# Value projections of a float32 transformer: 512 weight columns per matmul instead of 256

## The chip, the cores and the metric

The kernel runs on one core of a Trainium2 chip. The metric is device time in microseconds (us) from the start to the end of one execution. TensorE (PE) multiplies, VectorE (DVE) and ScalarE (ACT) do the elementwise work, GpSimd (POOL) some small steps, SyncE (SP) issues the loads. Matmul results land in PSUM, which has eight banks of 512 float32 columns on 128 partitions.

## The reference

One program of float32 work on x of 256 tokens by 1024 features. First a swiglu layer, token mixing and a second swiglu layer; then two blocks of attention and a squared-ReLU layer with layer norms, scaled and shifted by `c` through `ada_w`. The parts that the change touches are the projections to values:

```
# token mixing
rq, rk, rv, rg, nq, nk, nv, g_ret, g_na = split(u @ w_in, ...)   # rv 1024 wide, nv 512 wide
y    = bidirectional_retention(q, k, heads(rv, 256), ...)        # 4 heads
y_na = neighborhood_attention(nq, nk, nv, rel_bias) @ w_na_out   # 8 heads of 64
# first attention (16 heads of 64, causal; one block of 256 holds all tokens)
q, k, v = split(h @ w_in, 3)                                     # 1024 wide each
# second attention (8 heads, two maps of 64 each)
q, k, v = split(h @ w_in, 3)
w = softmax(q1 k1^T) - lam * softmax(q2 k2^T)
o = rms_norm(w @ v, subln_g) * (1 - lambda_init)                 # per head, 128 wide
out = o @ w_out
```

## The kernel before

Activations lie with features on the partitions, as X[128, 8, 256]: eight chunks of 128 features by 256 tokens. Every float32 operand is split into two float32r parts (H and L, or wh and wl), and one product becomes three: wh·XH, wh·XL, wl·XH (`mmA`, `mmB`).

Weights stream from DRAM in slots of 1 MB, each [128, 2048] in the buffer `raw`, four buffers deep, loaded by SP in one fixed order (the list `ws`). ScalarE copies half a slot to wh (L109), VectorE subtracts it for wl (L90); the halves lie in a ring of seven. The `tick()` after each half's products moves this stream on by a half and lets each waiting generator (`bg`) issue its next step: the heads of an attention are generators (`pair`), begun a number of ticks after their projection (`WAITS`, `NA_WAITS`, `RET_WAITS`). So the order on every engine is the order in which the program issues, and ticks are its clock.

Most projections (`proj`) hold weights still and move 256 tokens: the result has features on the partitions. Values are wanted with tokens on the partitions, so `projA` (L461) holds 128 tokens of X still and moves 256 weight columns. A slot has all 1024 rows of 256 columns; each half (512 rows) takes 24 products, for two token blocks, into the two halves of one bank. There are 14 such slots: four rv and two nv in mixing, four in each attention. ScalarE then copies the bank's two halves to SBUF (L1621 in the attentions), and `vdone` (`nvdone`) tells the heads that their values are there.

PSUM has two pools of four banks, `gu` and `acc`. Attention's pairs of heads take scores (as), transposed probabilities (at) in `acc`; the product with the values (ao) goes to a `gu` bank, or, once `tail` is set, to an `acc` bank, since the four banks of the output projection (oacc) take `gu` then. `QKV` sets the order of an attention's projections: (1, i) is queries and keys of two pairs of heads, (0, i) a slot of values. In the second attention a pair ends with Squares of ao on ScalarE (L1575), a sum s on VectorE (L545), a power r on POOL (L540), a product r and the scaled o on VectorE (L1579, L1581), two transposes of o on PE (L1585), and YH on ScalarE (L1591), YL on VectorE (L1592), the moving input's counterpart for the output projection (`down`, `down_tail`).

```
461  def projA(bank, XH, XL):
463      for h, (wh, wl) in enumerate(st.use(n, 256)):
466              for k in range(4):
467                  mmA(two(bank)[:, t], wh[:, k], wl[:, k], XH[:, 4 * h + k, ts], ...)
470          tick()
```

Of the kernel before, what the change touches and what calls it, by code (L numbers as in the profile page):

```python
# [16 lines left out]
D = 1024  # L17
# [16 lines left out]
# the order of the parts of an attention (1 for queries and keys, 0 for values; of which heads), after how  # L34
# many steps of the stream a pair of heads starts, and from which pair on two of its steps are one
QKV = (((1, 0), (0, 0), (0, 1), (1, 1), (1, 2), (1, 3), (0, 2), (0, 3)),
       ((1, 0), (0, 0), (1, 1), (1, 2), (0, 1), (1, 3), (0, 2), (0, 3)))
# [5 lines left out]
# the sums whose last products wait for the gap between two parts  # L43
# [6 lines left out]
class Stream:  # L50
    """Weights in the order of their use: loaded ahead, split into two float32r parts ahead."""
# [70 lines left out]
    def quarter(self, n, q):  # L122
        """A quarter of slot n, the first of which come before any others."""
        h, c = q // 2, slice(q % 2 * 512, q % 2 * 512 + 512)
        if q % 2 == 0:
            self.parts[n, h] = tuple(self.pool.tile([128, 1024], F32R, name=i, bufs=RING) for i in ("wh", "wl"))
        wh, wl = self.parts[n, h]
        raw = self.raw[n][:, q * 512:(q + 1) * 512]
        self.nc.scalar.activation(wh[:, c], raw, AF.Copy)  # L129
        return lambda: self.nc.vector.tensor_tensor(wl[:, c], raw, wh[:, c].bitcast(F32), OP.subtract)  # L130
# [10 lines left out]
    def ahead(self):  # L141
        """The next half of a slot, when it is a weight's."""
        if self.si in self.wpos and 2 * self.next_pos() < self.done + RING:
            self.piece(None)

    def use(self, n, b):
        """Slot n in two halves of its rows; each as its two parts, b columns wide."""
        while self.next_pos() <= n + 0.5:
            self.piece()
        self.flush()  # L150
        return [[t.rearrange("p (k f) -> p k f", f=b) for t in self.parts[n, h]] for h in range(2)]
# [10 lines left out]
def block_kernel(ctx, tc, A, out):  # L162
# [22 lines left out]
    def rev(t):  # L185
        """[128, 2, 256] of a tile, every 64 of a row backwards."""
        v = t[:, 63:64]
        return bass.AP(tensor=v.tensor, offset=v.offset, ap=[list(v.ap[0]), [S, 2], [64, 4], [-1, 64]])
# [4 lines left out]
    # ---- small tensors  # L193
# [31 lines left out]
    # ---- the order of the weights  # L225
    def cols(w, c0, k=KB, n=256):
        return ("w", w[:, c0:c0 + n].rearrange("(k p) f -> p k f", p=128), n)

# [28 lines left out]
    for i in range(2):  # L257
        ws.append(cols(wm, 256 * i))
        ws.append(cols(wm, 512 + 256 * i))
        for j in (2 * i, 2 * i + 1):  # L260
            ws.append(cols(wm, 1024 + 256 * j))
        for j in (2 * i, 2 * i + 1):
            ws.append(cols(wm, 2048 + 256 * j))
    for i in range(2):
        for b in (3072, 3584, 4096):
            ws.append(cols(wm, b + 256 * i))
    for i in range(4):
        ws.append(cols(wm, 4608 + 256 * i))
        ws.append(cols(A["w_ret_out"], 256 * i))
# [7 lines left out]
    for l, (wi, wo) in enumerate((("moba_w_in", "moba_w_out"), ("diff_w_in", "diff_w_out"))):  # L277
        for f, i in QKV[l]:
            for b in ((0, D) if f else (2 * D,)):
                ws.append(cols(A[wi], b + 256 * i))  # L280
        for i in range(4):
            ws.append(rws(A[wo], 256 * i))
        mlp_slots(A["mlp_w_up"][l], A["mlp_w_down"][l])
# [18 lines left out]
    # ---- adaLN modulation: columns of silu(c) @ ada_w + ada_b  # L302
# [24 lines left out]
    def ada_cols(o, t):  # L327
        """The sums over the partitions, of three bfloat16 parts that hold all of a float32."""
        pool, bufs = adap[-1]
        parts = [pool.tile([128, D], BF16, name=f"ada{i}", bufs=bufs) for i in range(3)]  # L330
        SC.activation(parts[0], t, AF.Copy)  # L331
        yield 1
        GP.tensor_tensor(t, t, parts[0], OP.subtract)  # L333
        yield 2
        SC.activation(parts[1], t, AF.Copy)
        yield 1
        GP.tensor_tensor(parts[2], t, parts[1], OP.subtract)
        ada_now.clear()
        ada_out.append((o, parts))
        if o // 8 in HELD:  # L340
            return
        yield 4
        ada_mm()
        yield 1
        ada_end()
# [3 lines left out]
    @contextmanager  # L349
    def ada_pool(n):  # L350
        """Room for the parts of n sums at once."""
        with tc.tile_pool(name="ada", bufs=1) as pool:
            adap.append((pool, n))
            yield
            ada_drain()
            ada_mm()
# [5 lines left out]
    def gap(p, n):  # L362
        """In the gap between two parts: products of a sum that waited for it, or of no use."""
        if ada_out:
            ada_mm(acc, 1)
            if not ada_out:
                start(ada_later(), 1)
            n -= 12
        warm(p, n)
# [48 lines left out]
    # ---- matrix products; a product of two float32 is three of their float32r parts  # L418
# [42 lines left out]
    def projA(bank, XH, XL):  # L461
        n = nxt()
        for h, (wh, wl) in enumerate(st.use(n, 256)):
            for t in range(2):
                ts = slice(t * 128, (t + 1) * 128)
                for k in range(4):
                    mmA(two(bank)[:, t], wh[:, k], wl[:, k], XH[:, 4 * h + k, ts], XL[:, 4 * h + k, ts],
                        h == 0 and t == 0 and k == 0, h == 1 and k == 3)
            st.release(n, h)
            tick()  # L470
# [35 lines left out]
    # ---- float32 into two float32r parts  # L506
# [4 lines left out]
    # ---- statistics over the features  # L511
    def stat(p):
        """What Stat left in a bank, by token."""
        return p[:, 0:128].rearrange("p (t c) -> p t c", c=64)[:, :, 0]

    class Stat:
        """Sums over the features of eight chunks, 64 like columns for 128 tokens; six of them are added up first."""
# [30 lines left out]
    def warm(p, n):  # L548
        """Products that nobody reads, for TensorE's clock not to fall while it waits."""
# [13 lines left out]
    class PostRms:  # L563
# [36 lines left out]
        def finish(self, coef, eps=RMS_EPS):  # L600
            """X += coef * rms_norm, by two chunks, and the next input of it."""
# [40 lines left out]
    class PostLn:  # L642
# [41 lines left out]
        def stats(self, means):  # L684
            """1/deviation by token; means(mean) once the mean is there."""
# [10 lines left out]
        def finish(self):  # L696
            """The next input, by two chunks, and what the residual needs: v - mean and 1/deviation."""
# [50 lines left out]
    class Ahead(PostLn):  # L748
        """A layer norm before products that take its input as x * a: what they lack is applied to their results."""
# [35 lines left out]
        def steps(self):  # L785
            """The statistics, the mean and 1/deviation by token on all partitions, the residual."""
# [21 lines left out]
        def proj(self, alloc):  # L808
            """x * a times 256 columns: the product, and that of -a and c."""
# [18 lines left out]
        def result(self, o, t):  # L828
            """The whole product but for what is to be added by feature."""
# [7 lines left out]
    class Last(PostLn):  # L837
        """The last layer norm: turned to tokens by rows before the statistics are known."""
# [83 lines left out]
    class Input:  # L922
        """The input of a part in two parts: x * a + c, a and c by feature."""
# [41 lines left out]
    class Next(Input):  # L965
        """The input of a part that normalizes after its first product: X * gain, and its statistics."""
# [37 lines left out]
    # ---- parts  # L1004
# [128 lines left out]
    # ---- start: x, transposed  # L1133
# [9 lines left out]
    def first_pair(banks, XH, XL):  # L1143
        """The first product, in the order in which its quarters come from DRAM."""
# [58 lines left out]
    # ---- token mixing  # L1203
    def mixing(nx):
        with tc.tile_pool(name="mix", bufs=1) as mp:
# [136 lines left out]
            for i in range(2):  # L1342
# [21 lines left out]
                for j in (2 * i, 2 * i + 1):  # L1364
                    b = gu("rv")
                    projA(b, XH, XL)
                    for t in range(2):
                        SC.activation(rv[:, t, j * 256:(j + 1) * 256], two(b)[:, t], AF.Copy, scale=nx.r[:, t:t + 1])
                    vdone.add(j)
# [9 lines left out]
            for i in range(2):  # L1379
# [10 lines left out]
                b = gu("nv")  # L1390
                projA(b, XH, XL)
                for t in range(2):
                    SC.activation(nv[:, t, i * 256:(i + 1) * 256], two(b)[:, t], AF.Copy, scale=nx.r[:, t:t + 1])
                nvdone.add(i)
# [53 lines left out]
    # ---- second block  # L1448
# [31 lines left out]
    def attention(l, nx, gate, follow):  # L1480
        with tc.tile_pool(name=f"att{l}", bufs=1) as mp:
# [115 lines left out]
            def room(n):  # L1597
                """Waits until n of the banks that products of attention go through are free."""
# [18 lines left out]
            def vv(i):  # L1617
                b = gu("v")
                projA(b, XH, XL)
                for t in range(2):  # L1620
                    SC.activation(vt[:, t, i * 256:(i + 1) * 256], two(b)[:, t], AF.Copy)  # L1621
                vdone.add(i)

            for f, i in QKV[l]:
                if not f and i == 2:
# [23 lines left out]
    def after_ln(l, i):  # L1649
        """The input of the part after a layer norm, and the residual from it."""  # L1650
# [89 lines left out]
```

## Time and profile before

| | us |
|---|---|
| median of three runs | 1287.78 (1287.3 to 1287.98) |
| profiled execution | 1287.8 |
| its span | 1287.8 |
| PE busy | 1262.7 (98%) |
| PE weight loads, beside the products | 1244.6 (97%) |
| VectorE busy | 1046.8 (81%) |
| ScalarE busy | 672.0 (52%) |
| POOL busy | 280.5 (22%) |

The profiled execution is one run of the program, and its span covers all of it. Busy times of an engine add up its instructions where they do not overlap. In the rows a PE product's own duration is longer than its step to the next one, since products overlap: 96 products with durations near 282 ns can take 11.39 us.

### The profile page before, as it was taken

Reading aid. Unit: us, or ns where it says so; the run is one execution under the profiler, and the core shown is the slowest. Engines: PE = TensorE matmul, PEld = TensorE weight load, DVE = VectorE, ACT = ScalarE, POOL = GpSimd, SP = SyncE. Lnnn points to the kernel's source line nnn. Section 1 sums busy time; section 2 is a strip of 40 time slices with the busy share of each in tenths; the row PEclk is TensorE's granted clock in tenths of the full one; section 3 lists DMA queues with packets and bytes.
Section 4 is the critical chain, followed back from the end, with each engine's and each line's share of the span. In section 5 each row is a group of like instructions: output and inputs, shape, how many; then the busy total and the mean of one; then the engine's idle time right before and its main releaser. Section 6 shows DMA issues by size and latency. Waiting matters only on the chain.

```text
span 1287.8 us, 25632 instructions
## 1 busy us (share of the span) xinstructions
PE 1262.7 (98%) x10768; PEld 1244.6 (97%) x10768; DVE 1046.8 (81%) x1437; ACT 672.0 (52%) x1070; POOL 280.5 (22%) x204
## 2 busy tenths in 40 slices
PE   9999999999999999999999999979999999999998
PEld 9999999999999999999999999979999999999997
DVE  5999867887776589887588759999969987998864
ACT  5454445656544365354465546545536565565542
POOL 1011104221000130011110017423322003832311
PEclk9999999999999999999999999989999999999999
DMA  8787974874566348877535335878753543677630
GB/s 300 264 309 256 317 244 90 268 240 149 200 226 212 116 164 301 303 279 262 164 111 186 131 99 188 270 271 281 260 171 113 183 132 103 225 250 234 202 134 33
DMA packets 176659, 265.25 MB, mean 206 GB/s; under 512 B 10432, under 2 KB 145952, under 8 KB 176544
## 3 DMA queue, kind: packets, MB, share of 16 engines
q1 hardware_dynamic: 169824, 261.53, 60.1%
q10 hardware_dynamic: 6720, 2.10, 0.9%
q8 instruction: 84, 1.38, 0.4%
q14 instruction: 31, 0.25, 0.1%
HBM read 262.56 MB, written 1.05 MB: 205 GB/s over the span
## 4 chain that ended last, share of the span: by engine, by line
PE 86%; DVE 8%; POOL 2%; issue 1%; ACT 1%; DMA 0%; DVEq 0%; SPq 0%; POOLq 0%; ACTq 0%
PE acc L191 24%; PE u L191 20%; PE g L191 12%; PE v L191 3%; PE q L191 3%; PE k L191 3%; PE oacc L191 2%; DVE wl L90 2%; PE yr L191 2%; PE rg L191 2%; PE rv L191 2%; PE as L191 1%; PE ao L191 1%; PE pst L191 1%; PE nk L191 1%
## 5 line engine op out<-in xcount | busy, mean ns | idle before, releaser
L90 DVE TENSOR_TENSOR wl<-raw,wh 128x1024 fp32r<-128x1024 f32 x392 | 515.2, 1334 | 24.3 <-ACT wh L109 23.9
L109 ACT ACTIVATE wh<-raw 128x1024 fp32r<-128x1024 f32 x392 | 403.6, 1052 | 130.3 <-PE u L191 32.2
L191 PE MATMUL acc<-HL,wh 128*128 128x256 f32 x864 | 243.9, 282 | 0.0
L191 PE MATMUL acc<-HH,wl 128*128 128x256 f32 x864 | 243.7, 282 | 0.0
L191 PE MATMUL acc<-HH,wh 128*128 128x256 f32 x864 | 242.8, 281 | 0.0
L191 PE MATMUL u<-XH,wh 128*128 128x258 f32 (+1 forms) x864 | 201.6, 285 | 0.4 <-ACT wh L129 0.4
L191 PE MATMUL u<-XL,wh 128*128 128x258 f32 (+1 forms) x864 | 200.7, 284 | 0.0
L191 PE MATMUL u<-XH,wl 128*128 128x258 f32 (+1 forms) x864 | 200.2, 283 | 0.0
L191 PEld LDWEIGHTS acc<-HH,wh 128*128 128x128 f32 x864 | 163.9, 190 | 0.0
L191 PEld LDWEIGHTS acc<-HH,wl 128*128 128x128 f32 x864 | 162.4, 188 | 0.0
L191 PEld LDWEIGHTS acc<-HL,wh 128*128 128x128 f32 x864 | 161.9, 187 | 0.0
L191 PEld LDWEIGHTS u<-XH,wh 128*128 128x128 f32 x864 | 145.7, 191 | 0.7 <-ACT wh L129 0.6
L191 PEld LDWEIGHTS u<-XH,wl 128*128 128x128 f32 x864 | 146.0, 191 | 0.1
L191 PEld LDWEIGHTS u<-XL,wh 128*128 128x128 f32 x864 | 145.1, 190 | 0.0
L191 PE MATMUL g<-XH,wh 128*128 128x256 f32 x480 | 133.5, 284 | 1.6 <-ACT XH L942 1.3
L191 PE MATMUL g<-XL,wh 128*128 128x256 f32 x480 | 133.2, 283 | 1.0 <-DVE XL L618 0.9
L191 PE MATMUL g<-XH,wl 128*128 128x256 f32 x480 | 132.7, 282 | 0.0
L320 DVE SCALAR_TENSOR_TENSOR adacc<-raw,csil,adacc 128x1024 f32<-128x1024 f32 x84 | 118.2, 1408 | 1.7
L834 POOL TENSOR_TENSOR a<-a,RB 128x512 f32<-128x512 f32 x32 | 68.0, 2125 | 170.7 <-DVE a L833 169.9
L333 POOL TENSOR_TENSOR adacc<-adacc,ada 128x1024 f32<-128x1024 f32 x12 | 27.7, 2311 | 329.3 <-ACT ada L331 254.3
L191 PEld LDWEIGHTS g<-XH,wh 128*128 128x128 f32 x480 | 89.5, 189 | 2.7 <-ACT XH L942 2.0
L191 PEld LDWEIGHTS g<-XL,wh 128*128 128x128 f32 x480 | 89.5, 189 | 1.6 <-DVE XL L618 1.1
(368 smaller groups left out, 2643.0 us busy)
## 6 DMA issues: line engine op xcount, KB each, us to landing
raw<-in_ada_w_dram SPq DMA_DIRECT2D x48, 1024.0 KB, 5.7
raw<-in_ffn_w_in_dram SPq DMA_DIRECT2D x42, 1024.0 KB, 6.8
raw<-in_mlp_w_up_dram SPq DMA_DIRECT2D x32, 1024.0 KB, 5.4
raw<-in_mlp_w_down_dram SPq DMA_DIRECT2D x32, 1024.0 KB, 5.0
raw<-in_w_mix_in_dram SPq DMA_DIRECT2D x26, 1024.0 KB, 5.6
raw<-in_ffn_w_out_dram SPq DMA_DIRECT2D x22, 1024.0 KB, 5.8
raw<-in_moba_w_in_dram SPq DMA_DIRECT2D x12, 1024.0 KB, 5.2
raw<-in_diff_w_in_dram SPq DMA_DIRECT2D x12, 1024.0 KB, 5.1
```

Source lines behind the costliest of these rows:

```text
L90: self.nc.vector.tensor_tensor(wl, raw, wh.bitcast(F32), OP.subtract)
L109: nc.scalar.activation(wh, self.raw[i][:, sl], AF.Copy)
L191: PE.matmul(o, l, r, start=start, stop=stop, skip_group_check=True)
L320: V.scalar_tensor_tensor(t, w, csil[:, kb:kb + 1], t, op0=OP.mult, op1=OP.add)
L333: GP.tensor_tensor(t, t, parts[0], OP.subtract)
L834: GP.tensor_tensor(two(t), two(t), bc2(self.R), OP.mult)
```

## The change

Values are now projected 512 columns at a time. A slot holds 512 rows by 512 columns (`wide`: two of them, one for each half of the rows, make 512 full columns). `projA` takes two banks, one for each block of 128 tokens, and two slots in a row; each half-slot (256 rows) is 12 products of 512 columns with a tick behind it. Both banks are evicted after the second slot, 512 columns at a time. The lists of weights follow. `QKV` names each half of the values once: in the first attention the values stand where they stood; in the second the second pair of old slots is moved. Mixing projects all nv after the first nq and nk. `tail` is set at the second half of the values. The lists `WAITS`, `ONE`, `RET_WAITS`, `NA_WAITS` and `HELD` are as before. Line numbers below `projA` are 9 higher.

```
-QKV = (((1, 0), (0, 0), (0, 1), (1, 1), (1, 2), (1, 3), (0, 2), (0, 3)),
-       ((1, 0), (0, 0), (1, 1), (1, 2), (0, 1), (1, 3), (0, 2), (0, 3)))
+QKV = (((1, 0), (0, 0), (1, 1), (1, 2), (1, 3), (0, 1)),
+       ((1, 0), (0, 0), (1, 1), (1, 2), (1, 3), (0, 1)))
...
+    def wide(w, c0):
+        return [("w", w[r:r + 512, c0:c0 + 512].rearrange("(k p) f -> p k f", p=128), 512) for r in (0, 512)]
...
-        for j in (2 * i, 2 * i + 1):
-            ws.append(cols(wm, 1024 + 256 * j))
+        ws.extend(wide(wm, 1024 + 512 * i))
...
-        for b in (3072, 3584, 4096):
+        for b in (3072, 3584):
             ws.append(cols(wm, b + 256 * i))
+        if i == 0:
+            ws.extend(wide(wm, 4096))
...
-            for b in ((0, D) if f else (2 * D,)):
-                ws.append(cols(A[wi], b + 256 * i))
+            if f:
+                ws.extend(cols(A[wi], b + 256 * i) for b in (0, D))
+            else:
+                ws.extend(wide(A[wi], 2 * D + 512 * i))
...
-    def projA(bank, XH, XL):
-        n = nxt()
-        for h, (wh, wl) in enumerate(st.use(n, 256)):
-            for t in range(2):
-                ts = slice(t * 128, (t + 1) * 128)
-                for k in range(4):
-                    mmA(two(bank)[:, t], wh[:, k], wl[:, k], XH[:, 4 * h + k, ts], XL[:, 4 * h + k, ts],
-                        h == 0 and t == 0 and k == 0, h == 1 and k == 3)
-            st.release(n, h)
-            tick()
+    def projA(banks, XH, XL):
+        for half in range(2):
+            n = nxt()
+            for h, (wh, wl) in enumerate(st.use(n, 512)):
+                for t in range(2):
+                    ts = slice(t * 128, (t + 1) * 128)
+                    for k in range(2):
+                        kk = 4 * half + 2 * h + k
+                        mmA(banks[t], wh[:, k], wl[:, k], XH[:, kk, ts], XL[:, kk, ts], kk == 0, kk == 7)
+                st.release(n, h)
+                tick()
...
-                for j in (2 * i, 2 * i + 1):
-                    b = gu("rv")
-                    projA(b, XH, XL)
-                    for t in range(2):
-                        SC.activation(rv[:, t, j * 256:(j + 1) * 256], two(b)[:, t], AF.Copy, scale=nx.r[:, t:t + 1])
-                    vdone.add(j)
+                bs = [gu("rv"), gu("rv")]
+                projA(bs, XH, XL)
+                for t in range(2):
+                    SC.activation(rv[:, t, i * 512:(i + 1) * 512], bs[t], AF.Copy, scale=nx.r[:, t:t + 1])
+                vdone.update((2 * i, 2 * i + 1))
...
-                b = gu("nv")
-                projA(b, XH, XL)
-                for t in range(2):
-                    SC.activation(nv[:, t, i * 256:(i + 1) * 256], two(b)[:, t], AF.Copy, scale=nx.r[:, t:t + 1])
-                nvdone.add(i)
+                if i == 0:
+                    bs = [gu("nv"), gu("nv")]
+                    projA(bs, XH, XL)
+                    for t in range(2):
+                        SC.activation(nv[:, t], bs[t], AF.Copy, scale=nx.r[:, t:t + 1])
+                    nvdone.update((0, 1))
...
             def vv(i):
-                b = gu("v")
-                projA(b, XH, XL)
+                bs = [gu("v"), gu("v")]
+                projA(bs, XH, XL)
                 for t in range(2):
-                    SC.activation(vt[:, t, i * 256:(i + 1) * 256], two(b)[:, t], AF.Copy)
-                vdone.add(i)
+                    SC.activation(vt[:, t, i * 512:(i + 1) * 512], bs[t], AF.Copy)
+                vdone.update((2 * i, 2 * i + 1))
...
-                if not f and i == 2:
+                if not f and i == 1:
                     tail.append(True)
```

How the instructions stand at three places of the second attention (ao: a pair's output bank; as: scores; oacc: the output projection; YH, YL: its input parts; s, r, o: a pair's scaling; cst: the identity of the transposes). The number behind a name tells buffers apart.

PE, last value tick of the second attention, before:

```order
L191 MATMUL v_12632<-wl_12316,XH_11425 128x256
L1585 MATMUL ao_12539<-cst_73,o_12543 128x128 x2
L191 MATMUL as_12684<-k_12628,q_12501 128x128
L191 MATMUL as_12685<-k_12628,q_12501 128x128
L191 MATMUL as_12684<-k_12628,q_12501 128x256
```

PE at the same place, now:

```order
L191 MATMUL v_12270<-wl_12100,XH_11175 128x512
L1594 MATMUL ao_12293<-cst_73,o_12297 128x128 x2
L191 MATMUL as_12400<-k_12265,q_12173 128x128
L191 MATMUL as_12401<-k_12265,q_12173 128x128
L191 MATMUL as_12400<-k_12265,q_12173 128x256
```

The products are twice as wide. The rows behind them keep their order, but ao_12539 lies in a `gu` bank and ao_12293 in an `acc` bank (bank 6), which as_12401 takes next.

PE, end of the second attention, before, from the last output product of one half-slot on:

```order
L191 MATMUL oacc_12868<-YH_11722,wl_12659 128x256
L1585 MATMUL ao_12948<-cst_73,o_12952 128x128 x2
L191 MATMUL ao_13003<-vt_11724,T_12960 128x128 x3
L191 MATMUL oacc_12865<-YH_11722,wh_12722 128x256
...
L191 MATMUL oacc_12868<-YH_11722,wl_12723 128x256
L1585 MATMUL ao_13003<-cst_73,o_13007 128x128 x2
L191 MATMUL oacc_12865<-YH_11722,wh_12771 128x256
```

PE at the same place, now:

```order
L191 MATMUL oacc_12469<-YL_11473,wh_12340 128x256
L191 MATMUL oacc_12469<-YH_11472,wl_12341 128x256
L1594 MATMUL ao_12554<-cst_73,o_12558 128x128 x2
L1594 MATMUL ao_12566<-cst_73,o_12570 128x128 x2
L1594 MATMUL ao_12626<-cst_73,o_12630 128x128 x2
L1594 MATMUL ao_12638<-cst_73,o_12642 128x128 x2
L191 MATMUL oacc_12466<-YH_11472,wh_12379 128x256
```

The transposes of the last two pairs stood 24 output products apart; now those of the last four pairs stand together behind the last products of a half-slot.

VectorE at this place, before:

```order
L545 TENSOR_SCALAR s_12956<-sa_12953 128x2
L90 TENSOR_TENSOR wl_12945<-raw_12533,wh_12944 128x1024
L1579 TENSOR_TENSOR r_12958<-r_12958,rs_12800 128x2
L1581 TENSOR_SCALAR o_12952<-ao_12948,r_12958 128x128 x2
L1592 SCALAR_TENSOR_TENSOR YL_11723<-ao_12948,sm_81,YH_11722 128x256
L545 TENSOR_SCALAR s_13011<-sa_13008 128x2
L90 TENSOR_TENSOR wl_12992<-raw_12661,wh_12991 128x1024
L1579 TENSOR_TENSOR r_13013<-r_13013,rs_12913 128x2
L1581 TENSOR_SCALAR o_13007<-ao_13003,r_13013 128x128 x2
L1592 SCALAR_TENSOR_TENSOR YL_11723<-ao_13003,sm_81,YH_11722 128x256
```

VectorE at the same place, now:

```order
L554 TENSOR_SCALAR s_12634<-sa_12631 128x2
L554 TENSOR_SCALAR s_12646<-sa_12643 128x2
L90 TENSOR_TENSOR wl_12616<-raw_12287,wh_12615 128x1024
L1601 SCALAR_TENSOR_TENSOR YL_11473<-ao_12554,sm_81,YH_11472 128x256
L1601 SCALAR_TENSOR_TENSOR YL_11473<-ao_12566,sm_81,YH_11472 128x256
L1588 TENSOR_TENSOR r_12636<-r_12636,rs_12512 128x2
L1590 TENSOR_SCALAR o_12630<-ao_12626,r_12636 128x128 x2
L1601 SCALAR_TENSOR_TENSOR YL_11473<-ao_12626,sm_81,YH_11472 128x256
L1588 TENSOR_TENSOR r_12648<-r_12648,rs_12519 128x2
L1590 TENSOR_SCALAR o_12642<-ao_12638,r_12648 128x128 x2
```

The YL of pairs 4 and 5 (ao_12554, ao_12566) now stand between the sums s and the scalings r and o of pairs 6 and 7.

## Rows read from the trace of the kernel before

**Rows 1.** The page's busy times by engine (share of the span).
```profile
PE 1262.7 (98%) x10768; PEld 1244.6 (97%) x10768; DVE 1046.8 (81%) x1437; ACT 672.0 (52%) x1070; POOL 280.5 (22%) x204
```
**Rows 2.** Chain of waits: start us, us, what.
```profile
662.03 11.39 PE v L191 x96
...
1112.60 5.76 PE acc L191 x48
1118.35 5.76 PE u L191 x48
```
**Rows 3.** Groups by form: operation, count, busy us, mean ns, idle before.
```profile
L191 PE MATMUL v<-wh,XH 128*128 128x256 f32 x128 | 36.7, 287 | 0.0
```
**Rows 4.** PE's timeline (start, us), and tile rows (ns min/median/max).
```profile
645.79 0.61 PE L191 MATMUL R<-identb 128*128 128x128 bf16 x8
...
1277.84 1.06 PE L191 MATMUL pst<-small,sq 128*128 128x64 f32 x8
1278.73 1.04 PE L863 MATMUL fo<-cst,X 128*128 128x128 f32 x8
1279.61 1.89 PE L191 MATMUL fo<-gb,dm 128*128 128x256 f32 x8
...
L191 PE MATMUL R<-identb x26: 216/218/219, 202.3 to 970.4; 128*128 128x128 bf16 x26
...
L191 PE MATMUL fo<-gb,dm x8: 379/379/382, 1279.6 to 1281.1; 128*128 128x256 f32 x8
```
**Rows 5.** Timelines of VectorE and PE in mixing; idle before in brackets.
```profile
221.67 3.48 DVE L90 TENSOR_TENSOR wl<-raw,wh 128x1024 fp32r<-128x1024 f32 x3
225.07 0.15 DVE L545 TENSOR_SCALAR s<-pst 128x2 f32<-128x2 f32 x1
...
226.96 0.71 PE L191 MATMUL R<-cst,r 128*128 128x128 f32 x4 [0.65 <-POOL r L540]
```
**Rows 6.** ScalarE's timeline, end of the second attention.
```profile
1070.29 0.47 ACT L1591 ACTIVATE YH<-ao,sm 128x256 fp32r<-128x256 f32 x1 [1.92 <-PE ao L1585]
...
1071.72 1.06 ACT L109 ACTIVATE wh<-raw 128x1024 fp32r<-128x1024 f32 x1
```
**Rows 7.** VectorE's timeline, the same stretch.
```profile
1070.79 0.48 DVE L1592 SCALAR_TENSOR_TENSOR YL<-ao,sm,YH 128x256 fp32r<-128x256 f32 x1 [1.04 <-ACT YH L1591]
...
1073.73 0.16 DVE L1579 TENSOR_TENSOR r<-r,rs 128x2 f32<-128x2 f32 x1 [0.58 <-POOL r L540]
1073.93 0.61 DVE L1581 TENSOR_SCALAR o<-ao,r 128x128 f32<-128x128 f32 x2
```
**Rows 8.** Evictions and exponentials of ScalarE: ns min/median/max, first and last start.
```profile
L587 ACT ACTIVATE sq<-acc x9: 597/598/599, 191.3 to 640.6; 128x512 f32<-128x512 f32 x9
...
L1621 ACT ACTIVATE vt<-v x16: 357/392/428, 668.8 to 1060.1; 128x256 f32<-128x256 f32 x16
...
L1520 ACT ACTIVATE P<-as,mx x64: 362/430/509, 680.8 to 1059.4; 128x128 f32<-128x128 f32 x32, 128x256 f32<-128x256 f32 x32
```
**Rows 9.** PE's timeline, the same stretch as rows 6.
```profile
1069.81 0.44 PE L1585 MATMUL ao<-cst,o 128*128 128x128 f32 x2 [0.76 <-DVE o L1581]
1070.09 0.83 PE L191 MATMUL ao<-vt,T 128*128 128x128 f32 x6
1070.67 0.37 PE L191 MATMUL oacc<-YH,wh 128*128 128x256 f32 x1
...
1074.59 0.44 PE L1585 MATMUL ao<-cst,o 128*128 128x128 f32 x2 [0.80 <-DVE o L1581]
```
**Rows 10.** PE's timeline, one piece of the chain, and windows (busy times, then PEclk).
```profile
839.64 0.19 PE L191 MATMUL adp<-small,ada 128*128 128x1 bf16 x2 [0.95 <-DVE cc L832]
845.46 0.74 PE L191 MATMUL adp<-small,ada 128*128 128x1 bf16 x22 [5.63 <-POOL ada L337]
...
846.20 5.14 PE u L191 x24
...
840.80:850.80 10.00, 5.34 (x44) 5.35 (x45) 9.96 (x8) 4.38 (x6) 4.60 (x2) 0.50 0.63 207
```

## Prediction

> **What bounds the kernel now.** Read the page's busy shares first [rows 1]: TensorE (PE) works 1262.7 of 1287.8 us, VectorE 1046.8, ScalarE 672.0. The chain of waits says the same: its long pieces are runs of matmuls with nothing between them [rows 2]. So an edit moves the time in two ways: through the pace of the products it touches, and through waits of PE that it makes or ends. The other engines count only where PE waits for them. The profiled span, 1287.8, is the run's whole time; the runs' median is 1287.78. The sum is made against 1287.8.
>
> **The products themselves.** There are 14 slots of values with 48 products each, 672 of 256 columns; the v group confirms it, with 128 wh·XH products in eight slots, a third of 8 x 48 [rows 3]. The change makes them 336 of 512. Before, 96 v products stand in 11.39 us of the chain [rows 2], 118.6 ns each.
>
> What does one of 512 columns take? No row shows one, so bound it.
> - Upper end, no gain: 2 x 118.6 = 237 ns.
> - Lower end, columns alone: eight bf16 products of 128 columns span .61 us [rows 4]. One of them lasts .218, so they follow each other by (.61 − .218) / 7 = 56 ns, at most .44 ns a column. At the full clock (1.00, 2.4 GHz) a column a pulse is .417 ns, 53 of the 56. By that 512 columns take 213, and with the 3 that are left 216.
> - Float32 products of 256 columns (fo<-gb,dm): eight span 1.89, one lasts .379, so 216 each [rows 4], .84 ns a column. A value product takes at most 118.6 / 256 = .46 a column. If float32 sends its columns through in two passes of .417, these 216 ns are 512 column steps in a row: once more 216.
> - Between: the 118.6 may be 107 of columns (.417 x 256) and 12 that every product pays. Then one of 512 takes 213 + 12 = 225.
>
> That something other than columns sets the pace at 256 is seen thrice: acc (256 columns) and u (258) take 5.76 per 48 both [rows 2]; and groups of eight float32 products of 64 and of 128 columns start .89 and .88 apart [rows 4], 111 and 110 ns each, twice the columns for nothing. Such a floor of 110 to 119 is gone under 213 of columns. I take 216, the value by two rows. The gain is 336 x (237 − 216) = 7.1 us; 4.0 at 225; 0 at 237.
>
> The Trainium skill ("TensorE: Matmul & The Clock Gate", "Back-to-back issue gap") gives an isolated product N/2.4 + 2.5 ns: 109 at 256 columns, where the row has 118.6, and 216 at 512. It also gives a sustained stream of load-and-product pairs about 131 ns at 512 columns; by that the gain would be 336 x (237 − 131) = 35.6 us. No run here shows such a rate.
>
> **What stands beside it at no cost.** The ring of weight halves advances after 12 products instead of 24, 2.6 us instead of 2.84; ScalarE's split of a half (1.06 [rows 6]) and VectorE's (3.48 / 3 = 1.16 [rows 5]) still go under that. ScalarE's evictions become two of 512 columns in place of four of 256: .598 (another 512-column read of a bank) against .392 each [rows 8], 0.4 less per pair, on an engine 52% busy. The slots are 512 rows by 512 columns, still one transfer of 1 MB.
>
> **Mixing: the wait for R.** PE waits .65 at 226.96 for r [rows 5], which comes from VectorE's s at 225.07, behind three wl splits. Both halves of products ahead of it become shorter, r does not come earlier, so the wait takes back most of the gain there: two ticks of 12 by 21 ns, .5 us. **+0.5** (0 to .5).
>
> **The second attention's scores.** In the last value tick the order now puts pair 3's transposes (ao_12293) right ahead of two score products, the second of which (as_12401) goes to the same bank. That bank is free when ScalarE and VectorE have read the transposes. For another pair this took from 1069.81 [rows 9], where the transposes start, to 1071.27, where YL ends [rows 7]: 1.46. PE fills .28 of it with the transposes (1069.81 to the next group's start at 1070.09 [rows 9]) and .1 with the first score product. Before, ao_12539 was in another bank than the scores behind it. **+1.1** (0 to 1.5).
>
> **The end of the second attention.** Here the order changes most. Before, the last pairs' transposes come one pair at a time, 24 output products apart, and each waits for its own scaling: .76 at 1069.81 and .80 at 1074.59 [rows 9], with what PE takes to get going again 1.9 together. The change gives the pairs fewer steps behind the last values: the transposes of pairs 4 to 7 stand in a row after the fourth group of 24 output products, and VectorE has YL of 4 and 5 ahead of r and o of pair 6, and YL of 6 ahead of r and o of pair 7.
>
> Walk it from t = 0 where PE starts pair 6's products with the values. A pair's six take .58 (1070.09 [rows 9] to the output products' start at 1070.67), two pairs 1.2; 24 output products at 120 (5.76 / 48) end at 4.1; the transposes of 4 and 5, .28 each, at 4.65. ScalarE starts YH of 4 .48 after its transposes (1069.81 to 1070.29 [rows 6, 9]), VectorE YL .50 later, .48 each [rows 7]: YL of 4 ends at 5.55, YL of 5 at 6.05. Then r and o of pair 6, 1073.73 to 1074.54, .8 [rows 7]: the transposes of 6 start at 6.9, a wait of 2.2. Its YL ends 1.46 later, at 8.35; r and o of 7 end at 9.15; the transposes of 7 start at 9.2, and PE has waited since 7.2, 2.0. Together some 4.3 against 1.9: **+2.4** (0, if scalings and YL come as they did, to 3). The powers r of 6 and 7 on POOL I take to be over by then: the Squares they need can start at t = .6, and VectorE has waited for POOL's r until 1073.73, 3.6 after that pair's products began at 1070.09 [rows 7, 9]; here it is after 6 us that r is wanted.
>
> **Evictions behind the last values.** The third and fourth output bank are those of the value products. ScalarE has exponentials of the last pairs (.36 to .51 [rows 8]) ahead of the two evictions; one of them in the way is about **+0.5** (0 to .8).
>
> **The clock.** Once before PE stood for .95 and 5.63 with two small products between [rows 10]; in the 10 us behind 840.8 the granted clock is .50 (1.2 GHz). 24 u products took 5.14 there [rows 10] against 2.88 (half of 5.76): 2.3 us lost. The waits of .76 and .80 brought no drop. Two of about 2 within 4.6 us lie between. I take that it falls once behind them, and that products at half clock are as many as there: **+2.2** (0 to 2.3).
>
> **Sum.** −7.1 + .5 + 1.1 + 2.4 + .5 = −2.6; with the clock −.4: 1287.8 − .4 = **1287.4**. The bounds: 1280.7 with 7.1 gained and no new wait; 1295.9 with nothing gained and each wait at its upper end (.5 + 1.5 + 3 + .8 + 2.3 = 8.1).
>
> **Rivals.**
> - The clock holds. For it: the waits of .76 and .80 brought no fall [rows 9], and PE works between the two new ones. −2.6: 1285.2.
> - The waits at the end stay as they were, and so does the clock. For it: an order tells no times; a split that comes earlier would let VectorE do the scalings in time. −7.1 + .5 + .5, with or without the 1.1: 1281.7 to 1282.8. Against: YL of 4 and 5 can't start before their transposes, and these stand behind the 24 products whatever VectorE does.
> - The wide products are dearer than 216; this one ends on the slower side. At 237 nothing is gained and .5 + 1.1 + 2.4 + .5 + 2.2 = 6.7 are lost: 1294.5; at 225 1290.5. It decides from 237 − 6.7 / .336 = 217 ns on. For it: 118.6 is more than the 110 of the floor rows, and no row says what the rest is paid for.
> - PE takes in weights beside the running product so well that 131 ns are enough: 1287.8 − 35.6 + 6.7 = 1258.9. Against: the bf16 row has no column under .417 [rows 4], so 512 no less than 213. The page named above has this rule.
>
> **How the numbers follow.** A measurement of this kernel can tell 0.2%, 2.6 us, from no change: faster is below 1285.2, slower above 1290.4. Chances: the forecast .42; the clock holds .20; waits as before .12; dearer products .23 (225 .15, 237 .08); the rate of 131 .01; anything else .02. Faster: .05 of the forecast's spread, half of the clock's case (.10), .12, .01 and .02: .30. Slower: .05 of the forecast's spread, .17 of the dearer products, .01: .23. Same: .47. The range of 8 in 10 goes from the waits as before, 1281.8, to between 225 and 237, 1292. The forecast's own range is 1285.5 to 1289.5.
>
> **What would show it.** The step from one v product to the next (216, 225 or 237), and the 96 products' 11.39, now 48 in 10.4; about .65 + .5 of waiting before R near 227; as waiting once for YL in the second attention's last value tick; two waits of about 2 us in front of transposes at its end, and the granted clock in the 10 us behind them. The prediction is wrong if those two waits are no longer than the .76 and .80, if the clock holds behind them, or if the step is not 216.

## The result, and the profile after

The changed kernel takes 1296.01 us, median of four runs (1295.30 to 1297.12), against 1287.88 of the kernel before (1287.30 to 1289.02). The ratio is 1.0064, 95% interval 1.005 to 1.0078: 8.1 us slower. The prediction had 1287.4 and a range of 1281.8 to 1292.

The profiled execution of after has a span of 1294.9 and took 1296.7, so 1.8 us lie outside the span; in the runs since it is 1.7 to 2.8, mostly 1.8. That the span "is the run's whole time" was wrong: the execution profiled before, with its span of 1287.8, will by this estimate have taken about 1289.6, more than the highest of its four runs here. Runs of one kernel lie in two groups some 1.5 us apart (before 1287.3 to 1288.0 and 1289.0, after 1295.3 and 1296.7 to 1297.1), and both profiled executions are of the upper one. So 7.1 between the two spans and 8.1 between the medians go together.

The page's busy times and the chain's piece of value products, answering [rows 1] and [rows 2]:

```profile
PE 1263.8 (98%) x10432; PEld 1229.3 (95%) x10432; DVE 1047.0 (81%) x1437; ACT 670.8 (52%) x1056; POOL 280.1 (22%) x204
```

```profile
662.22 11.13 PE v L191 x48
```

PE's products are 336 fewer, but its busy time is 1.1 us longer. The 48 wide v products take 11.13 us where 96 narrow ones took 11.39: 231.9 ns each, not 216. Two narrow ones took 237.3 (2 x 11.39 / 96). Over 336 products that is 336 x (237.3 − 231.9) = 1.8 us gained.

PE's timeline in mixing, at the last value step of the second attention, and at its end (start, us, instruction, idle before and what ended it), answering [rows 5] and [rows 9]:

```profile
227.42 0.71 PE L191 MATMUL R<-cst,r 128*128 128x128 f32 x4 [0.77 <-POOL r L549]
...
1050.54 0.38 PE L1594 MATMUL ao<-cst,o 128*128 128x128 f32 x2
1050.85 0.49 PE L191 MATMUL as<-k,q 64*128 64x128 f32 x2
1052.00 0.92 PE L191 MATMUL as<-k,q 64*128 64x128 f32 x6 [0.67 <-DVE YL L1601]
...
1072.72 0.60 PE L1594 MATMUL ao<-cst,o 128*128 128x128 f32 x4
1077.95 0.69 PE L1594 MATMUL ao<-cst,o 128*128 128x128 f32 x2 [4.64 <-DVE o L1590]
1080.44 0.69 PE L1594 MATMUL ao<-cst,o 128*128 128x128 f32 x2 [1.79 <-DVE o L1590]
```

Of the predicted waits all but the one for the evictions are there: R .77 instead of .65, as .67, and two at the end. The first of these is 4.64, where the prediction's walk had 2.2. What PE waits for is o of pair 6. ScalarE and VectorE in that stretch, answering [rows 6] and [rows 7]:

```profile
1066.68 1.10 ACT L109 ACTIVATE wh<-raw 128x1024 fp32r<-128x1024 f32 x1
1073.19 0.37 ACT L1584 ACTIVATE o<-ao,rs 128x128 f32<-128x128 f32 x1 [5.41 <-PE ao L1594]
...
1074.57 1.07 ACT L109 ACTIVATE wh<-raw 128x1024 fp32r<-128x1024 f32 x1
1075.52 0.85 ACT L1600 ACTIVATE YH<-ao,sm 128x256 fp32r<-128x256 f32 x2
```

```profile
1074.72 0.17 DVE L554 TENSOR_SCALAR s<-sa 128x2 f32<-128x2 f32 x1 [0.53 <-ACT o L1584]
1075.17 1.23 DVE L90 TENSOR_TENSOR wl<-raw,wh 128x1024 fp32r<-128x1024 f32 x1 [0.28 <-issue]
1076.31 0.87 DVE L1601 SCALAR_TENSOR_TENSOR YL<-ao,sm,YH 128x256 fp32r<-128x256 f32 x2
1077.10 0.15 DVE L1588 TENSOR_TENSOR r<-r,rs 128x2 f32<-128x2 f32 x1
1077.29 0.61 DVE L1590 TENSOR_SCALAR o<-ao,r 128x128 f32<-128x128 f32 x2
```

ScalarE stood 5.41 us before the first Square of pair 6, and what released it is a transpose of PE at L1594. The Squares' input had been there since the two pairs' products with the values ended: the output products behind them start at 1069.76. But the Square writes the tile `o` (it is its scratch), `o` has two buffers, and those hold the scaled outputs of pairs 4 and 5 until these are transposed at 1072.72. Behind the late Squares come s, ScalarE's split, VectorE's split, YL of 4 and 5, then r and o.

Then the clock. Windows of 4 us (busy times by engine, then the granted clock):

```profile
1070.00:1074.00 4.00, 3.32 (x29) 3.08 (x27) 0.00 (x0) 0.81 (x5) 0.00 (x0) 1.00 0.54 191
1074.00:1078.00 4.00, 0.05 (x1) 0.05 (x1) 3.03 (x8) 2.36 (x7) 1.38 (x2) 0.80 0.01 2
1078.00:1082.00 4.00, 2.21 (x10) 1.80 (x11) 1.49 (x5) 1.31 (x5) 0.00 (x0) 0.50 0.01 2
1082.00:1086.00 4.00, 4.00 (x30) 4.00 (x30) 2.33 (x6) 1.25 (x3) 0.00 (x0) 0.85 0.31 75
```

It falls to .50 (1.2 GHz) while PE stands, and is back between 1082 and 1086. The last 96 output products run from the first oacc product to the first u product behind them; PE's rows for the two, before:

```profile
1074.79 0.36 PE L191 MATMUL oacc<-YH,wh 128*128 128x256 f32 x1
...
1086.38 0.41 PE L191 MATMUL u<-XH,wh 128*128 128x258 f32 x2
```

and after:

```profile
1080.78 0.56 PE L191 MATMUL oacc<-YH,wh 128*128 128x256 f32 x1
...
1093.45 0.40 PE L191 MATMUL u<-XH,wh 128*128 128x258 f32 x2
```

Before takes 11.59 us, after 12.67: 1.1 us. The transposes just ahead of them lie in the low clock too: at 1077.95 and 1080.44 two follow each other by .27, in before by .17.

The sum of the two traces, by the start times of like instructions. After is .5 later at 12 us, ahead of every change; .1 earlier at the first value product of the second attention (983.82 against 983.92); 1.4 earlier at its first output product (1057.10 against 1058.49); 6.0 later at the first of the last 96 (1080.78 against 1074.79); 7.1 later at u. The 1.4 is for the most part no gain, and the 7.4 behind it is not all loss: 18 products of one pair (12 with the values, 6 transposes of probabilities, at some .11 each 2.0 us) stand ahead of the first output product in before and behind it in after. What the end costs is read from the waits for o: 4.64 and 1.79, 6.43 together, against .76 and .80, 1.56. That is 4.9 net; the .5 that is left goes to starting again behind the waits and to transposes at the low clock. On the other side, the products' 1.8 can't be followed to the tenth: between 339 and 643 us, where nothing was changed, the two traces move apart by .3.

### The profile page after: what moved, and what is told of

Read it like the earlier page. It is cut to its first block, busy times and chain, and to the rows that moved or that the text cites. A ratio compares the mean times of both kernels' runs of the same rounds, so it can differ in the third digit from the quotient of the medians.

```text
span 1294.9 us, 24949 instructions
## 1 busy us (share of the span) xinstructions
PE 1263.8 (98%) x10432; PEld 1229.3 (95%) x10432; DVE 1047.0 (81%) x1437; ACT 670.8 (52%) x1056; POOL 280.1 (22%) x204
## 4 chain that ended last, share of the span: by engine, by line
PE 86%; DVE 9%; issue 2%; POOL 1%; ACT 1%; DMA 0%; SPq 0%; DVEq 0%; POOLq 0%; ACTq 0%
PE acc L191 24%; PE u L191 20%; PE g L191 12%; PE v L191 3%; PE q L191 3%; PE k L191 3%; PE oacc L191 3%; DVE wl L90 2%; PE yr L191 2%; PE rg L191 2%; PE as L191 1%; PE rv L191 1%; PE ao L191 1%; PE pst L191 1%; PE nq L191 1%
```

## Experiments

Theory A, from the trace: nearly all of the loss stands at the end of the second attention, where transposes of four pairs are in a row, and the wait there is made longer by the two buffers of `o`; the products themselves gain 1.8 us. Rivals: the waits are VectorE's order alone (B); they are a pair's own scaling latency wherever it stands (C); wide products or their late eviction cost time in all stages.

**The buffers.** e_o4:

```
-                o = mp.tile([128, S], F32, name="o", bufs=2)
+                o = mp.tile([128, S], F32, name="o", bufs=4)
```

> The kernel after, with four buffers instead of two for the tile o of the second attention. Theory A (the Squares of pairs 6 and 7 write o and so wait until the transposes of pairs 4 and 5 have read it; that makes the wait 4.6 instead of the 2.2 of the prediction's walk): the Squares start right behind their products, r is ready before YL of 4 and 5 ends, the two waits of PE fall from 4.6 and 1.8 to about 2.2 and 2.0, the kernel after gets 2 to 3 us faster, about 1293.5. Theory B (the waits are VectorE's order, splits and YL ahead of the scalings, whatever the buffers): waits and time stay, 1296.

Measured: 1294.15 (1293.39 to 1295.35), ratio to before 1.0043 (1.003 to 1.0057), so 1.9 us less than after by the medians. This interval and that of after overlap; what the buffers do is read from the trace. ScalarE's first Square of pair 6 and PE's transposes:

```profile
1069.51 0.37 ACT L1584 ACTIVATE o<-ao,rs 128x128 f32<-128x128 f32 x1 [1.59 <-PE ao L191]
```

```profile
1072.86 0.60 PE L1594 MATMUL ao<-cst,o 128*128 128x128 f32 x4
1075.43 0.44 PE L1594 MATMUL ao<-cst,o 128*128 128x128 f32 x2 [1.97 <-DVE o L1590]
1077.66 0.69 PE L1594 MATMUL ao<-cst,o 128*128 128x128 f32 x2 [1.80 <-DVE o L1590]
```

The Square is now released by the products with the values, and the wait of 4.64 is 1.97. B falls for the first wait: 2.7 of it were the buffers. What is left is what the prediction had walked to, 3.8 together against 1.6 in before. The clock took part of the gain back, in windows as above:

```profile
1074.00:1078.00 4.00, 0.78 (x4) 0.54 (x5) 2.50 (x9) 0.59 (x2) 0.00 (x0) 0.85 0.01 2
1078.00:1082.00 4.00, 4.00 (x21) 4.00 (x20) 1.78 (x4) 1.61 (x4) 0.00 (x0) 0.50 0.08 11
1082.00:1086.00 4.00, 4.00 (x29) 4.00 (x29) 0.87 (x2) 1.43 (x3) 0.46 (x1) 0.79 0.66 255
```

PE came back to work earlier, and the low clock now lay on products instead of on waiting: the 96 output products took 14.07 us (1078.00 to 1092.08), 2.5 more than the 11.59 of before.

**The transposes in a row.** e_one lets pairs 4 and 5 go without the step between their scaling and their transposes:

```
-ONE = ((7, 8), (8, 6))
+ONE = ((7, 8), (8, 4))
```

> The kernel after, with the last number of ONE 4 instead of 6: the transposes of pairs 4 and 5 come one step earlier, 24 output products ahead of those of 6 and 7. Theory A (the loss is the four pairs' transposes in a row, by way of o's buffers): the waits of 4.6 and 1.8 shrink to .3 and at most .8, the clock holds, the time falls by 6 to 7.5 us to about 1289. Theory C (the scaling's own latency of VectorE, POOL and VectorE is what PE waits for, wherever the transposes stand): both waits move, 2 us or more stay in each, 1292 to 1296.

Measured: 1291.21 (1290.40 to 1292.84), ratio 1.0023 (1.0014 to 1.0032): 4.8 less than after, not 6 to 7.5. PE's transposes:

```profile
1066.20 0.38 PE L1594 MATMUL ao<-cst,o 128*128 128x128 f32 x2
1068.38 0.44 PE L1594 MATMUL ao<-cst,o 128*128 128x128 f32 x2 [1.79 <-DVE o L1590]
...
1073.19 0.44 PE L1594 MATMUL ao<-cst,o 128*128 128x128 f32 x2 [0.17 <-DVE o L1590]
1075.43 0.44 PE L1594 MATMUL ao<-cst,o 128*128 128x128 f32 x2 [1.80 <-DVE o L1590]
```

VectorE between the last two of these:

```profile
1074.17 0.48 DVE L1601 SCALAR_TENSOR_TENSOR YL<-ao,sm,YH 128x256 fp32r<-128x256 f32 x1 [1.04 <-ACT YH L1600]
```

The first pair of each two hardly waits, the second waits 1.8. So C is wrong, and A was incomplete: a pair that follows another in the same step has its r and o (here at 1074.57 and 1074.76) behind the other's YL on VectorE, and that YL waits for ScalarE's YH and so for the first pair's transposes. Before, the last pairs stood one to a step. The clock stayed at 1.00 with these waits, and the 96 output products took 11.60.

**The second pair's place.** e_defer has ONE as e_one, four buffers of `o`, and holds the transposes, YH and YL of such pairs back until every pair of the step has issued its scaling:

```
+        while ends:                       # last lines of bg()
+            ends.pop(0)()
...
-                for c in range(2):
-                    PE.transpose(two(p)[:, c, 128:256], two(o)[:, c], ident)
...
+                if l and j >= ONE[l][1]:
+                    ends.append(end)      # end(): transposes, YH, YL, live[0] -= late
+                else:
+                    end()
```

> The kernel e_one (last number of ONE 4) with four buffers of o, and the transposes, YH and YL of a tail pair held back until all pairs of that step have issued their scalings. Theory D (what is left in e_one are second pairs that stand behind the first one's YL on VectorE, 2.1 per stacked pair): the gaps of 2.07, .44 and 2.07 in front of transposes shrink to .3 each at most, the time falls by 3.5 to 4 us against e_one, about 1287.5, level with before or slightly below. Theory C (latency of a pair's own scaling): the gaps stay, 1291.

Measured: 1288.86 (1287.57 to 1290.17), ratio 1.0001 (.9992 to 1.001).

```profile
1068.90 0.60 PE L1599 MATMUL ao<-cst,o 128*128 128x128 f32 x4
1073.11 0.44 PE L1599 MATMUL ao<-cst,o 128*128 128x128 f32 x2 [0.74 <-DVE o L1594]
1073.83 0.44 PE L1599 MATMUL ao<-cst,o 128*128 128x128 f32 x2 [0.27 <-DVE o L1594]
```

The waits of 1.8 are gone; .74 and .27 remain, more than the .3 expected. The time is 2.4 us less than e_one's, not 3.5 to 4, and 7.2 less than after's, with the wide products and the order of the weights unchanged: the end of the second attention was the loss. That the four buffers, and not the new place, ended the waits of 1.8 is a rival that e_one's trace goes against: with two buffers its Squares of pair 6 are already released by the products with the values (1069.58), and the second pair's o follows the first one's YL.

**The second attention left alone.** e_l1old has wide products in mixing and in the first attention; the second attention has the slots, the order and the 256-column products of before:

```
-       ((1, 0), (0, 0), (1, 1), (1, 2), (1, 3), (0, 1)))
+       ((1, 0), (0, 0), (1, 1), (1, 2), (0, 1), (1, 3), (0, 2), (0, 3)))
...
+            elif l:
+                ws.append(cols(A[wi], 2 * D + 256 * i))
...
-                (qk if f else vv)(i)
+                (qk if f else vv1 if l else vv)(i)     # vv1, with before's projA
```

> Products of 512 columns in mixing and in the first attention alone; the second attention has the order, the slots and the 256-column products of before. Theory A (all of the loss stands at the end of the second attention): 20 half-slots gain .06 to .07 each, 1.3 us, less .2 at R: about 1 us faster than before, 1287.3. A theory in which wide products or their late eviction cost time wherever they are: part of the 8 us stays, 1290 or more.

Measured: 1288.32 (1286.49 to 1289.38), ratio .9996 (.9987 to 1.0005). The loss is gone, which the theory of a cost everywhere did not allow. Of the 1 us expected the times show .5, not clear of nothing. Between the two traces, from 12 us to the transposes at 1067, it gains 1.1 us on before by the start times of like instructions; .3 of it lie in the second attention, where nothing differs, so this is no closer than some tenths.

**The width alone.** e_narrow keeps after's slots and order, with every wide product as two of 256 columns:

```
-                        mmA(banks[t], wh[:, k], wl[:, k], XH[:, kk, ts], XL[:, kk, ts], kk == 0, kk == 7)
+                        for c in range(2):
+                            cs = slice(c * 256, c * 256 + 256)
+                            mmA(banks[t][:, cs], wh[:, k, cs], wl[:, k, cs], XH[:, kk, ts], XL[:, kk, ts],
+                                kk == 0 and c == 0, kk == 7)
```

> The kernel after, order and slots unchanged, but each product of 512 columns written as two of 256 into the two halves of the bank (672 products again). By the pace read from the trace after (232 ns against 2 x 118.6): 336 x 5 = 1.7 us slower than after, about 1297.7. By the prediction's pace (216), if other losses hid it: 7 us slower, 1303. If columns alone set the pace: no change, 1296.

Measured: 1298.12 (1295.67 to 1298.78), ratio 1.0066 (1.0053 to 1.0079); after has 1.0064. The times exclude the 7 us of the predicted pace, and do not tell 1.7 from nothing. The trace does: its chain's piece of value products, and the waits of PE for o (us in total, times, longest):

```profile
661.14 11.36 PE v L191 x96
```

```profile
PE ao L1597 <- DVE o L1593: 6.4, 2, 4.6
```

Two narrow products take 236.7 ns there (2 x 11.36 / 96), where one wide takes 231.9. And the same two waits stand in front of the last transposes without any wide product: the order makes them.

**The pace by itself.** e_pace and e_pace2 run strings of products that nobody reads behind the kernel's end, with all other engines and loads still, then beside them:

```
+    def string(name, n, cols, ...):
+        p = acc(name)
+        for i in range(n):
+            mm(p[:, 0:cols], w0[:, 128 * (i % 4):128 * (i % 4) + 128], w1[:, 512:512 + cols], i == 0, i == n - 1)
```

> The kernel after with strings of unread products behind its end: 60 and 24 float32r products of 512 columns, 48 of 256, 48 of 128, 24 bf16 of 512, all with VectorE, ScalarE and loads still; then 36 of 512 beside VectorE subtracts, 36 beside ScalarE copies, 72 of 512 and 48 of 256 beside four 1 MB loads. P1 (each product pays some 12 to 18 ns over its columns): 232 at 512 and 119 at 256 throughout. P2 (the other engines' reads of SBUF slow the moving columns): 216 at 512 and 109 at 256 in the still strings, 232 and 119 beside the engine or the loads that cause it. P3 (float32r passes a column in .453 ns by itself): 232, 118 and 60 in the still strings, bf16 216.

The chain's pieces (start us, us, what, count): qa float32r 512 columns, qb 256, qc 128, qd bf16 512, all still; qe (512) beside VectorE, qf ScalarE, qg loads.

```profile
1308.00 5.44 PE qa L191 x24
1313.44 5.75 PE qb L191 x48
1319.19 5.31 PE qc L191 x48
1324.50 5.20 PE qd L191 x24
1329.70 8.17 PE qe L191 x36
1337.87 8.16 PE qf L191 x36
1346.03 16.32 PE qg L191 x72
```

227 ns at 512 columns, 120 at 256, 111 at 128; 217 for bf16 at 512; and 227 beside each kind of traffic. Neither P2 nor P3. P1 has it, with 13 ns, though not its 232. The string of 256 columns that was meant for the loads ran behind their end.

> The kernel after with other strings of unread products behind its end: float32r of 512 columns that alternate between two moving tiles, 48 of 384, 48 of 192, bf16 of 256 and of 128, and 60 of 512 and 60 of 256 beside VectorE, ScalarE and loads all at once. If each float32r product pays 13.4 ns over its columns (e_pace: 227 at 512, 120 at 256): 173 at 384, 111 at 192 (the floor), bf16 109 and 56 to 60. If the other 5 ns of the value products (232) come from the three streams together: 232 beside them. If they come from changing the moving tile: 232 in the first string.

qb is float32r of 384 columns, qc of 192, qd bf16 of 256, qe of 128; qg is 512 columns beside VectorE, ScalarE and loads together, for some 10 of its 13.6 us.

```profile
1315.57 8.34 PE qb L191 x48
1323.91 5.34 PE qc L191 x48
1329.25 5.25 PE qd L191 x48
1334.50 2.68 PE qe L191 x48
...
1342.71 13.60 PE qg L191 x60
```

174, 111, 109 and 56. A column takes .417 ns at 2.4 GHz, so float32r pays 13 to 14 ns over its columns at 256, 384 and 512 and takes 111 at 128 and at 192, a floor; bf16 pays 2.5 to 3.3. All traffic at once leaves 227.

e_pace3 came nearer to a value product step by step:

> The kernel after with strings of 48 unread float32r products of 512 columns behind its end, that come nearer to a value product one by one: one stationary and one moving tile; two stationary tiles in turn (H, L, H); two moving tiles too (H, H, L); two banks in turn every six products; then 96 of 256 columns with all of it. If one of these makes the step of the value products (232 and 118.5, uneven from product to product), it changes from 227 (even) to 232 in the string where it comes in, and 256 columns from 120 to 118.5. If none: 227 in all, and the 5 ns come from something else in the kernel.

227 in all strings of 512 columns, 120 in that of 256. The value products' own 232, and 118.5 at 256, are not explained: in the kernel the steps of 512 columns are uneven (226 to 239), in the strings even (225 to 228).

**Two that missed.** e_o4warm was to keep PE busy in e_o4's two waits:

```
+                if l and j >= ONE[l][1]:
+                    for _ in range(36 - 4 * (j - 6)):
+                        mm(two(p)[:, 0, 128:256], identb, identb, True, True)
```

> The kernel e_o4 with 36 and 32 unread bf16 products ahead of the transposes of pairs 6 and 7, some 2.0 and 1.8 us of work in waits of 2.2 and 2.1. If the fall of the clock is a cost of its own: the 96 output products behind it take 11.6 us instead of 14.1, and the time falls by 2.4 us to about 1291.7. If the clock falls for another reason: 1294 to 1294.5.

Measured: 1296.70 (1295.81 to 1298.60), ratio 1.0064 (1.005 to 1.0078), 2.6 us more than e_o4. The fillers write into the bank that o is computed from, so the wait went to the first of them and they ran behind it:

```profile
1074.43 3.30 PE L191 MATMUL ao<-identb 128*128 128x128 bf16 x36 [1.97 <-DVE o L1590]
...
1079.95 1.95 PE L191 MATMUL ao<-identb 128*128 128x128 bf16 x32 [1.79 <-DVE o L1590]
```

They took the low clock upon themselves (36 in 3.30 us, 92 ns each, against the second 32 in 1.95), and the 96 output products behind took 11.60 again. What a filled wait saves was not measured: all eight banks are in use there.

e_waits starts pairs 4, 5 and 7 a step earlier in e_defer:

```
-WAITS = ((4, 5, 4, 3, 0, 5, 2, 1), (6, 5, 2, 4, 4, 4, 0, 2))
+WAITS = ((4, 5, 4, 3, 0, 5, 2, 1), (6, 5, 2, 4, 3, 3, 0, 1))
```

> The kernel e_defer with the starts of pairs 4, 5 and 7 of the second attention one step earlier (WAITS 3, 3, 0, 1): pairs 4 to 6 come a step earlier, only pair 7 has its transposes behind the last group of 24 output products, and pair 3's transposes no longer stand ahead of scores in the same bank. Theory A and D together (what is left of the loss are waits for scalings and for the bank): the gaps of 1.0, .5 and .9 go, 1.7 us less than e_defer, about 1287.1, .1% under before. If the earlier scores make PE wait for VectorE in the value steps instead: 1289 or more.

Measured: 1291.88 (1289.71 to 1292.71), ratio 1.0021 (1.0012 to 1.003). The end is better, with one wait of .5 for o, but the value steps now hold scores that wait for exponentials:

```profile
1043.37 0.48 PE L191 MATMUL as<-k,q 64*128 64x128 f32 x2 [1.37 <-ACT P L1533]
...
1050.68 0.92 PE L191 MATMUL as<-k,q 64*128 64x128 f32 x6 [1.35 <-ACT P L1533]
```

No version ran clearly below before. e_l1old and e_defer are level with it. So the 1.8 us that the products gain stand in the steps of the traces, and no run's time shows them.

## Why the prediction was wrong

- **The products**: the step "I take 216, the value by two rows" failed. It took the 3 ns over the columns from a bf16 row, and read the 118.6 of 256 columns as a floor that wide products leave. The strings show a floor of 111 at 128 and 192 columns, and above it columns plus 13 for float32r. The case "107 of columns and 12 that every product pays" was in the text as the middle value and was right for the strings: 225 against 227. The kernel's own step is 231.9, so the gain was 1.8 us instead of 7.1: 5.3 of the 8.6 us between forecast and result. The Trainium skill's isolated gap (N/2.4 + 2.5, "TensorE: Matmul & The Clock Gate", "Back-to-back issue gap") holds for the bf16 strings (217, 109, 56) and not for float32r; its sustained 131 at 512 was met by no string.
- **The end of the second attention**: the place was right, and the order of VectorE's work too; the size was not. The step that failed is "the Squares they need can start at t = .6": they waited for the buffers of `o`, and ScalarE stood 5.41 us. The waits for o came to 6.43 against 1.56, 4.9 net, instead of 2.4. e_o4 has the walk's own conditions and shows 1.97 and 1.80 where the walk had 2.2 and 2.0.
- **R, as, evictions**: R cost .1 instead of .5, since wide products shorten the steps ahead of it by 2%, not 9%. as waited .67 instead of 1.1. No wait for the evictions shows (.5 predicted).
- **The clock**: it fell, as forecast, and cost 1.1 on the output products instead of 2.2, because PE stood for much of the low stretch. In e_o4, with less waiting, it cost 2.5.
- The rival on the slower side, dearer products, ends at 1290.5 for 225. It was nearer to the pace, and it too came out low, since it shared the walk: by its own rule even the measured 231.9 gives 1287.8 − 1.8 + 6.7 = 1292.7.

With the measured sizes the sum is −1.8 + .1 + .7 + 4.9 + 1.1 = 5.0, and 5.5 with the .5 of restarts and of transposes at the low clock, beside 7.1 between the spans. Of the 1.6 left, .5 is there at 12 us, and some .6 is gain that the start times ahead of the second attention don't show (.6 instead of the 1.2 that the steps give there, net of R); the rest stays open.

## What to carry to other kernels

When an order is rewritten, follow each buffer as well as each engine: an instruction that was early enough by its inputs can wait for the reader of an older buffer, and a scratch output (here a Square's) counts as a writer. Where two chains of the same kind are issued one behind the other on in-order engines, issue all first stages before any last stage, or the second chain waits for the whole of the first. Take a product's price from rows of its own type.

## What the runs showed of the hardware

In the strings at granted clock 1.00 a float32r product took 111 ns at 128 and 192 columns, 120 at 256, 174 at 384 and 227 at 512; bf16 56, 109 and 217 at 128, 256 and 512. At granted clock .50 (e_pace, 1292 to 1296 us) float32r products of 512 columns took 427 each: 512 columns at 1.2 GHz (426.7) and nothing over it. VectorE, ScalarE and loads beside them left the 227 of 512 columns as it was. And a shorter wait can cost more clock: 12.67 us for 96 products behind waits of 4.64 and 1.79, 14.07 behind 1.97 and 1.80.
